# Every third expert row combined in three float32r products, with G built in chunks of 52, 24 and 52 rows

## The chip, the core and the metric

The kernel runs on one core of a Trainium2 chip. The metric is the device time of one launch in microseconds (us). The kernel is one program whose instructions stand in a fixed order on each engine: TensorE (PE in the profile; PEld are its weight loads), VectorE (DVE), ScalarE (ACT), GpSimd (POOL) and SyncE (SP), the last of which issues most DMA transfers. Each engine works through its own list in order and waits on semaphores for the others.

## The reference

Two layers of an encoder work on 512 tokens of width 1024. Each layer has a mixer (attention, a short convolution and a stick-breaking head group) and then a layer of experts; the change lies in the experts. Cut to what matters:

```python
PEER_HEADS, PEER_N_KEYS, PEER_TOPK = 8, 128, 16      # 128 * 128 experts
s1, s2 = scores of two half queries against 128 keys each
top_s, experts = the best 16 of the sums s1 + s2, for each token and head
g = softmax(top_s)
act = gelu(einsum('tkd,td->tk', u_tab[experts], h))   # experts = i1 * 128 + i2
out = einsum('tk,tkd->td', g * act, v_tab[experts])
x   = layer_norm(alpha * x + (1 + gate2) * out)
```

So each token has 8 x 16 = 128 chosen experts out of 16384, each with a row of u and a row of v of 1024 float32 numbers.

## The kernel before

The 512 tokens are four blocks of 128. Two of them (DENSE = 1 and 2, 256 tokens together) compute all 16384 experts, and a table G, which is zero except for a token's chosen experts, keeps those that count. The other two (0 and 3) fetch their chosen rows one by one. Both ways run at the same time, and that stretch is the dense part of a layer.

**The dense blocks** (`dense`, L724 to L885) walk over 128 expert rows; expert row a holds the 128 experts with i1 = a. For each row:

- `load_u` (L801) loads 128 x 1024 numbers of u (512 KB, issued by SyncE), TensorE transposes them in eight pieces into PSUM (L810), ScalarE rounds each half to float32r (`uh`, L812) and VectorE takes the rest (`ul`, L814). A float32r operand holds the leading part of a float32 number.
- `scores` (L819) forms the scores of the row's 128 experts for 256 tokens as a sum over eight pieces of three float32r products each (L824 to L826): high by high, high by low, low by high. ScalarE applies gelu (L828) and VectorE multiplies by G's row (L830); the result is `w` (the tile is named ge).
- `load_v` (L833) loads 512 KB of v.
- `combine` (L839) adds w times v to four PSUM accumulators of 128 x 512 (L842). These four matmuls have float32 operands. A float32 matmul stands in the trace as two records, so a row has eight.

The row loop (L862) emits the transposes of row a + 1, the scores of row a, and the combine of row a - 1, so a combine runs one row behind its scores. The tile v has two buffers: the load of a row's v can start when the combine two rows before is done.

**The table G** is made by `build` (L773). A build covers 8 tokens of one chunk of rows: VectorE makes one-hot tiles of i2 (L781, 1024 elements) and of i1 (L785, 8 x n elements for a chunk of n rows), and multiplies the latter by three parts of g (L790, three times); TensorE joins them in 24 small bf16 matmuls (L797); ScalarE copies the result into G (L799). 256 tokens are 32 builds for a chunk. CUTS sets the chunks: 43, 42 and 43 rows. Two buffers hold G, so a chunk is built while the chunk before it is used: chunk 0's builds stand ahead of row 0; `coming` (L847) spreads chunk 1's 32 builds evenly over rows 0 to 42, and chunk 2's over rows 43 to 84. Rows 85 to 127 have no builds. From chunk 1 on, a build's PSUM tile takes turns with the transposes in two buffers (tag "ut").

**The other blocks** (`experts`, L673) fetch 128 rows at a time with an indirect DMA that GpSimd issues (512 KB a gather, four buffers, L689 and L701). VectorE multiplies and sums each gathered tile of u with h (L691) and adds each gathered tile of v, weighted, to an accumulator (L706).

**What sets the order.** A scheduler orders the instructions of every engine when the program is built. The main loop (L935 to L951) hands it the expert sums in pace with the dense rows: after each row's mark (`held`, the last VectorE instruction of its scores or build) some 2.7 expert sums follow in layer 0 and 2.9 in layer 1, and one after each of chunk 0's builds. On VectorE, expert sums, u's remainders, builds and the gating products thus stand in one list.

Of the kernel before, what the change touches and what calls it, by code (L numbers as in the profile page):

```python
# [11 lines left out]
F32 = mybir.dt.float32  # L12
F32R = mybir.dt.float32r
# [4 lines left out]
OP = mybir.AluOpType  # L18
# [3 lines left out]
P = 128  # L22
D = 1024
# [7 lines left out]
PH, NK, TOPK = 8, 128, 16  # L31
TG = 8
TI = 2
CUTS = (0, 43, 85, 128)
DENSE = (1, 2)
EARLY = (80, 110)
LATE = (50, 0)
# [15 lines left out]
def body(ctx, tc, x, c, positions, ada_w, ada_b, w_in, q_norm_g, kv_norm_g, w_uq, w_ukv, conv_w,  # L53
         w_o, ln1_g, ln1_b, peer_wq, peer_k1, peer_k2, peer_u, peer_v, ln2_g, ln2_b, out):
    nc = tc.nc
# [668 lines left out]
    def dense(y, blocks, res):  # L724
        l = y.l
        st = ExitStack()
        dw = st.enter_context(tc.tile_pool(name=f"dw{l}", bufs=1))
        dps = st.enter_context(tc.tile_pool(name=f"dps{l}", bufs=1, space=PSUM))
        TD = 2 * P
# [36 lines left out]

        NCH = len(CUTS) - 1
        WIDE = max(b - a for a, b in zip(CUTS, CUTS[1:]))
        held = [None]
# [3 lines left out]
        def build(ch, t0):  # L773
            c0, c1 = CUTS[ch], CUTS[ch + 1]
            n = c1 - c0
# [43 lines left out]
        def scores(a, us):  # L819
# [9 lines left out]
            ch = chunk_of[a]  # L829
            held[0] = nc.vector.tensor_tensor(ge, ge, G[ch][:, a - CUTS[ch], :], op=OP.mult)  # L830
            return ge

        def load_v(a):  # L833
# [2 lines left out]
            nc.sync.dma_start(v, v_flat[e0:e0 + NK, :])  # L836
            return v

        def combine(a, w, v):  # L839
            for g in range(2):  # L840
                for i in range(2):
                    nc.tensor.matmul(acc[i][g], lhsT=w[:, i * P:(i + 1) * P], rhs=v[:, g * 512:(g + 1) * 512],  # L842
                                     start=a == 0, stop=a == NK - 1)

        chunk_of = [ch for ch in range(NCH) for _ in range(CUTS[ch], CUTS[ch + 1])]

        def coming(a):  # L847

            ch = chunk_of[a]
            if ch + 1 == NCH:  # L850
                return ch + 1, range(0)
            k, n, m = a - CUTS[ch], CUTS[ch + 1] - CUTS[ch], TD // TG
            return ch + 1, range(k * m // n * TG, (k + 1) * m // n * TG, TG)

        for t0 in range(0, TD, TG):
            build(0, t0)
            yield held[0]
        acc = [[dps.tile([P, 512], F32, name=f"acc{i}{g}", tag=f"acc{2 * i + g}", bufs=1) for g in range(2)]
               for i in range(2)]
        us = load_u(0)  # L860
        w = {}
        for a in range(NK + 1):  # L862
            if a < NK:
                un = load_u(a + 1) if a + 1 < NK else None
                w[a] = scores(a, us)
                us = un
                ch, groups = coming(a)
                for t0 in groups:
                    build(ch, t0)
            if a > 0:  # L870
                combine(a - 1, w.pop(a - 1), load_v(a - 1))
            if a < NK:
                yield held[0]
# [19 lines left out]
    for l in range(L):  # L893
# [40 lines left out]
        res[3] = partial(pick, 3, *h[1:])  # L934
        A.stack.close()  # L935
        dn = dense(y, DENSE, res)
        ex = chain.from_iterable(experts(y, b, *res[b]) for b in range(NB) if b not in DENSE)
        pace(ex, None, EARLY[l])
# [35 lines left out]
```

## Time and profile before

| | us |
|---|---|
| median of three runs | 3543.99 |
| lowest and highest | 3531.81, 3545.16 |
| profiled execution | 3547.72 |
| its span, first to last instruction | 3546.0 |
| TensorE busy in it | 3074.8 |
| VectorE busy in it | 2754.8 |
| ScalarE busy in it | 928.7 |
| GpSimd busy in it | 1456.3 |

Busy is the time in which at least one instruction of the engine ran; on TensorE matmuls overlap, so its pace is better read from the step between the starts of two matmuls. The dense part is the stretch from 671 to 1770 us in layer 0 and from 2421 to 3517 us in layer 1. Its stages below are bounded by the starts of combines: 776.0 is the combine of row 0, 918.7 that of row 16, 1196.6 of row 51, 1389.4 of row 75, and 1770.0 the end of row 127's; in layer 1 row 75's combine stands at 3140.9 and row 127's ends at 3517.2.

### The profile page before, as it was taken

The page shows a single profiled execution, that of the slowest core. Times are in us where ns is not written, and L with a number is a line of the kernel's source. Part 1 is how long each engine was busy: PE and PEld are TensorE (multiplying, and loading weights), DVE is VectorE, ACT ScalarE, POOL GpSimd, SP SyncE. Part 2 cuts the span into 40 slices and gives each one's busy share as a digit, 9 for nine tenths or more (in the row PEclk, how much of TensorE's full clock was granted, in tenths as well). Part 3 has the DMA queues.
Part 4 walks back from the last instruction along what each step waited for, and adds up shares of the span by engine and source line. Part 5 has one row for each costly group of instructions (what it writes and reads, how often), then busy time and mean ns, then how long its engine had stood idle before and what let it go on. Part 6 is the DMA issues. An engine that isn't in the chain of part 4 may idle for free.

```text
span 3546.0 us, 51872 instructions
## 1 busy us (share of the span) xinstructions
PE 3074.8 (87%) x18364; PEld 2019.4 (57%) x18364; DVE 2754.8 (78%) x6213; ACT 928.7 (26%) x1859; POOL 1456.3 (41%) x1347
## 2 busy tenths in 40 slices
PE   7878879659999999999948987785789999999998
PEld 2433434436777777777724444444567767677775
DVE  3667897999777877677675578889998887776777
ACT  2342432222222222222222223312222222222221
POOL 1034563256433434444451144534454444434443
PEclk9989989859999999999969997896799999999998
DMA  8767968558888888899885577794779988889997
GB/s 290 239 206 256 329 227 305 173 192 289 301 325 304 314 308 320 305 343 350 330 296 198 171 273 259 261 325 155 245 275 344 338 309 318 314 323 335 361 352 255
DMA packets 340051, 1011.98 MB, mean 285 GB/s; under 512 B 40504, under 2 KB 53064, under 8 KB 339792
## 3 DMA queue, kind: packets, MB, share of 16 engines
q0 software_dynamic: 147456, 536.94, 42.5%
q1 hardware_dynamic: 192336, 471.73, 38.2%
q8 instruction: 146, 2.39, 0.3%
q14 instruction: 113, 0.93, 0.1%
HBM read 1002.06 MB, written 6.34 MB: 284 GB/s over the span
## 4 chain that ended last, share of the span: by engine, by line
PE 15%; DVE 12%; DMA 10%; issue 9%; POOL 3%; ACT 1%; DVEq 0%; POOLq 0%; ACTq 0%
DMA g<-in_peer_v,eidx 5%; PE acc L842 4%; PE pm L154 3%; DMA g<-in_peer_u,eidx 3%; DVE g L691 2%; DVE acc L706 2%; POOL g L689 2%; PE sp L824 1%; PE sp L825 1%; PE sp L826 1%; DVE tk_ef L661 1%; PE utp L810 1%; POOL g L701 1%; DVE o L790 1%; DVE o L781 1%
## 5 line engine op out<-in xcount | busy, mean ns | idle before, releaser
L701 POOL DMA_INDIRECT g<-in_peer_v,eidx x512 | 613.7, 1199 | 802.2 <-DVE acc L706 486.4
L842 PE MATMUL acc<-v,ge 128*128 128x512 f32 x2048 | 927.1, 595 | 6.8 <-DVE ge L830 6.7
L689 POOL DMA_INDIRECT g<-in_peer_u,eidx x512 | 593.0, 1158 | 755.8 <-DVE g L691 508.5
L706 DVE SCALAR_TENSOR_TENSOR acc<-g,wts,acc 128x1024 f32<-128x1024 f32 x508 | 668.8, 1316 | 143.0 <-DMA g<-in_peer_v,eidx 139.6
L691 DVE SCALAR_TENSOR_TENSOR g<-g,h 128x1024 f32<-128x1024 f32 x512 | 619.7, 1225 | 180.8 <-DMA g<-in_peer_u,eidx 180.2
L824 PE MATMUL sp<-hh,uh 128*128 128x256 f32 x2048 | 613.7, 300 | 1.1 <-ACT ge L828 1.1
L826 PE MATMUL sp<-hh,ul 128*128 128x256 f32 x2048 | 595.0, 291 | 0.0
L825 PE MATMUL sp<-hl,uh 128*128 128x256 f32 x2048 | 584.5, 285 | 0.0
L842 PEld LDWEIGHTS acc<-v,ge 128*128 128x128 f32 x2048 | 370.1, 190 | 372.0 <-issue 364.3
L812 ACT CAST uh<-utp 128x512 fp32r<-128x512 f32 x512 | 303.3, 594 | 911.7 <-PE utp L810 772.6
L814 DVE TENSOR_TENSOR ul<-utp,uh 128x512 fp32r<-128x512 f32 x512 | 346.5, 684 | 106.9 <-ACT uh L812 106.4
L824 PEld LDWEIGHTS sp<-hh,uh 128*128 128x128 f32 x2048 | 392.9, 192 | 6.1 <-issue 4.1
L825 PEld LDWEIGHTS sp<-hl,uh 128*128 128x128 f32 x2048 | 393.1, 192 | 4.6 <-issue 4.5
L826 PEld LDWEIGHTS sp<-hh,ul 128*128 128x128 f32 x2048 | 391.9, 191 | 0.1
L810 PE MATMUL utp<-ident,u 128*128 128x128 f32 x2048 | 304.9, 278 | 57.0 <-DVE ul L814 54.0
L810 PEld LDWEIGHTS utp<-ident,u 128*128 128x128 f32 x2048 | 237.4, 142 | 136.0 <-issue 66.4
L799 ACT COPY G<-pg 128x344 f32<-128x344 f32 (+1 forms) x192 | 146.4, 763 | 561.8 <-PE pg L797 557.9
L797 PE MATMUL pg<-o,o 128*128 128x43 bf16 (+1 forms) x4608 | 182.5, 190 | 97.7 <-DVE o L790 85.4
L797 PEld LDWEIGHTS <-o 128*128 128x128 bf16 x4608 | 162.6, 102 | 179.9 <-issue 84.5
L154 PE MATMUL pm<-wt,hT 128*128 128x512 f32 (+1 forms) x512 | 231.3, 601 | 24.2 <-DMA wt<-in_w_in 13.4
L154 PE MATMUL pm<-wt,h2T 128*128 128x512 f32 x512 | 238.2, 611 | 8.8 <-DMA wt<-in_peer_wq 8.2
L660 POOL TENSOR_TENSOR tk_pick<-tk_hot,tk_ce 128x400 f32<-128x400 bf16 x128 | 125.7, 982 | 153.6 <-DVE tk_hot L658 151.7
(234 smaller groups left out, 3259.9 us busy)
## 6 DMA issues: line engine op xcount, KB each, us to landing
u<-in_peer_u SPq DMA_DIRECT2D x256, 512.0 KB
v<-in_peer_v SPq DMA_DIRECT2D x256, 512.0 KB
wt<-in_peer_wq SPq DMA_DIRECT2D x128, 512.0 KB
adw<-in_ada_w SPq DMA_DIRECT2D x160, 256.0 KB
wt<-in_w_o SPq DMA_DIRECT2D x64, 512.0 KB
wt<-in_w_in SPq DMA_DIRECT2D x48, 512.0 KB
wt<-in_ada_w SPq DMA_DIRECT2D x16, 512.0 KB
g<-in_peer_u,eidx POOLq DMA_INDIRECT x512, 7.0
```

Of the source, the lines that this page charges most:

```text
L154: r = nc.tensor.matmul(pm[:, :n], lhsT=lhsT[:, k0 + k, :], rhs=wt[:, k, :n], start=k0 + k == 0, stop=k0 + k == KT - 1)
L689: nc.gpsimd.indirect_dma_start(out=g, out_offset=None, in_=u_flat, in_offset=bass.IndirectOffsetOnAxis(ap=eidx[:, h, k:k + 1], axis=0))
L691: after(nc.vector.scalar_tensor_tensor(out=g, in0=g, scalar=1.0, in1=h2, op0=OP.mult, op1=OP.mult, accum_out=dots[:, h, k:k + 1]))
L701: nc.gpsimd.indirect_dma_start(out=g, out_offset=None, in_=v_flat, in_offset=bass.IndirectOffsetOnAxis(ap=eidx[:, h, k:k + 1], axis=0))
L706: r = nc.vector.scalar_tensor_tensor(out=acc, in0=g, scalar=wts[:, h, k:k + 1], in1=acc, op0=OP.mult, op1=OP.add)
L797: nc.tensor.matmul(pg[:, tt, 0:n], lhsT=o2[:, tt // TI, :, tt % TI], rhs=o1a[:, tt // TI, p, 0:n, tt % TI], start=tt == 0 and p == 0, stop ...
L810: nc.tensor.transpose(pt[:, j * P:(j + 1) * P], u[:, k * P:(k + 1) * P], ident)
L814: nc.vector.tensor_tensor(ul.rearrange("p j t -> p (j t)"), pt, uh.rearrange("p j t -> p (j t)").bitcast(F32), op=OP.subtract)
L824: nc.tensor.matmul(sp, lhsT=uh[:, j, :], rhs=hh[:, k, :], start=k == 0, stop=False)
L825: nc.tensor.matmul(sp, lhsT=uh[:, j, :], rhs=hl[:, k, :], start=False, stop=False)
L826: nc.tensor.matmul(sp, lhsT=ul[:, j, :], rhs=hh[:, k, :], start=False, stop=k == KT - 1)
L842: nc.tensor.matmul(acc[i][g], lhsT=w[:, i * P:(i + 1) * P], rhs=v[:, g * 512:(g + 1) * 512], start=a == 0, stop=a == NK - 1)
```

## The change

Two things change.

First, CUTS becomes (0, 52, 76, 128): G's chunks are 52, 24 and 52 rows wide. Each still takes 32 builds. Chunk 1's now stand in rows 0 to 51, chunk 2's in rows 52 to 75. A build of a chunk of 52 has 416 elements in its i1 tiles, one of 24 rows 192; before there were 344 or 336.

Second, for rows a with a % 3 == 1 (1, 4, ..., 127: 43 in each layer) `combine` splits w and v into a float32r high part (a copy on ScalarE) and a float32r remainder (a subtraction on VectorE), and replaces each of the four float32 matmuls by three float32r products, high by high, high by low and low by high, as the scores have them. The eight new tiles have one buffer each.

```diff
-CUTS = (0, 43, 85, 128)
+CUTS = (0, 52, 76, 128)
...
+        def split(src, shape, tag):
+            hi = dw.tile(shape, F32R, name="hi", tag=tag, bufs=1)
+            nc.scalar.copy(hi, src)
+            lo = dw.tile(shape, F32R, name="lo", tag=tag + "lo", bufs=1)
+            nc.vector.tensor_tensor(lo, src, hi.bitcast(F32), op=OP.subtract)
+            return hi, lo
+
         def combine(a, w, v):
+            if a % 3 == 1:
+                wh, wl = split(w, [P, TD], "wh")
+                vh, vl = split(v, [P, D], "vh")
+                for g in range(2):
+                    vs = slice(g * 512, (g + 1) * 512)
+                    for i in range(2):
+                        ws = slice(i * P, (i + 1) * P)
+                        nc.tensor.matmul(acc[i][g], lhsT=wh[:, ws], rhs=vh[:, vs], start=False, stop=False)
+                        nc.tensor.matmul(acc[i][g], lhsT=wh[:, ws], rhs=vl[:, vs], start=False, stop=False)
+                        nc.tensor.matmul(acc[i][g], lhsT=wl[:, ws], rhs=vh[:, vs], start=False, stop=a == NK - 1)
+                return
```

The new lines move later ones down: L842 becomes L860, and the new instructions carry L841 (the copies), L843 (the subtractions) and L854 to L856 (the products). The scheduler then orders everything anew.

TensorE, a split row in the second half of layer 0's dense part; acc_6139 to acc_6142 are the four accumulators, u is being transposed at L810. Before:

```order
L826 MATMUL sp<-hh,ul 128x256
L842 MATMUL acc_6139<-v,ge 128x512
L842 MATMUL acc_6141<-v,ge 128x512
L842 MATMUL acc_6140<-v,ge 128x512
L842 MATMUL acc_6142<-v,ge 128x512
L810 MATMUL utp<-ident,u 128x128 x8
```

Now:

```order
L854 MATMUL acc_6139<-hi 128x512
L855 MATMUL acc_6139<-lo,hi 128x512
L856 MATMUL acc_6139<-hi,lo 128x512
L854 MATMUL acc_6141<-hi 128x512
L855 MATMUL acc_6141<-lo,hi 128x512
L856 MATMUL acc_6141<-hi,lo 128x512
L854 MATMUL acc_6140<-hi 128x512
L855 MATMUL acc_6140<-lo,hi 128x512
L856 MATMUL acc_6140<-hi,lo 128x512
L854 MATMUL acc_6142<-hi 128x512
L855 MATMUL acc_6142<-lo,hi 128x512
L856 MATMUL acc_6142<-hi,lo 128x512
```

Four matmuls became twelve between the same neighbours: scores ahead, transposes behind.

VectorE, two rows from the gating product of one (L830) to that of the next but one, around row 58 of layer 0; o with a number are one-hot tiles, 4x86 and 4x104 their four groups of 43 or 52 rows by two tokens. Before:

```order
L830 TENSOR_TENSOR ge<-ge,G 128x256
L781 TENSOR_TENSOR o_11527<-iotab,i2T 128x1024
L785 TENSOR_TENSOR o_11529<-iotab,i1T 128x4x86
L691 SCALAR_TENSOR_TENSOR g,dots<-g,h_10865 128x1024
L790 TENSOR_TENSOR o_11529<-o_11529,gT 128x4x86 x3
L814 TENSOR_TENSOR ul<-utp,uh 128x512 x2
L830 TENSOR_TENSOR ge<-ge,G 128x256
L691 SCALAR_TENSOR_TENSOR g,dots<-g,h_10865 128x1024 x4
L814 TENSOR_TENSOR ul<-utp,uh 128x512
L691 SCALAR_TENSOR_TENSOR g,dots<-g,h_10865 128x1024
L814 TENSOR_TENSOR ul<-utp,uh 128x512
L830 TENSOR_TENSOR ge<-ge,G 128x256
```

Now, the later part of the same stretch:

```order
L781 TENSOR_TENSOR o_11688<-iotab,i2T 128x1024
L785 TENSOR_TENSOR o_11690<-iotab,i1T 128x4x104
L691 SCALAR_TENSOR_TENSOR g,dots<-g,h_10955 128x1024
L843 TENSOR_TENSOR lo<-ge,hi 128x256
L814 TENSOR_TENSOR ul<-utp,uh 128x512
L790 TENSOR_TENSOR o_11690<-o_11690,gT 128x4x104 x3
L814 TENSOR_TENSOR ul<-utp,uh 128x512
L830 TENSOR_TENSOR ge<-ge,G 128x256
L781 TENSOR_TENSOR o_11721<-iotab,i2T 128x1024
L785 TENSOR_TENSOR o_11723<-iotab,i1T 128x4x104
L790 TENSOR_TENSOR o_11723<-o_11723,gT 128x4x104 x3
```

One build in two rows became two whole builds, wider ones, with a split's subtraction among them.

VectorE, one row around row 91 of layer 0, where no builds stand. Before:

```order
L830 TENSOR_TENSOR ge<-ge,G 128x256
L706 SCALAR_TENSOR_TENSOR acc<-g,wts,acc 128x1024 x3
L814 TENSOR_TENSOR ul<-utp,uh 128x512 x2
L830 TENSOR_TENSOR ge<-ge,G 128x256
L706 SCALAR_TENSOR_TENSOR acc<-g,wts,acc 128x1024 x3
```

Now:

```order
L830 TENSOR_TENSOR ge<-ge,G 128x256
L706 SCALAR_TENSOR_TENSOR acc<-g,wts,acc 128x1024
L843 TENSOR_TENSOR lo<-ge,hi 128x256
L706 SCALAR_TENSOR_TENSOR acc<-g,wts,acc 128x1024
L843 TENSOR_TENSOR lo<-v,hi 128x1024
L706 SCALAR_TENSOR_TENSOR acc<-g,wts,acc 128x1024
L814 TENSOR_TENSOR ul<-utp,uh 128x512 x2
L830 TENSOR_TENSOR ge<-ge,G 128x256
```

The two subtractions of a split stand between expert sums, ahead of the remainders of u.

## Rows read from the trace of the kernel before

**Rows 1.** The profile's first line: the span and the number of instructions.

```profile
span 3546.0 us, 51872 instructions
```

**Rows 2.** Combine matmuls (L842) by stage: length, busy us (records) of TensorE.

```profile
918.70:1196.60 277.90, 126.31 (x281) 50.27 (x282) 0.99 0.86 311
1196.60:1389.40 192.80, 87.28 (x192) 34.33 (x193) 1.00 0.87 315
1389.40:1770.00 380.60, 187.63 (x416) 75.15 (x417) 1.00 0.90 332
```

**Rows 3.** Stages: length; busy us; granted clock, DMA share, GB/s.

```profile
core 0: us, PE busy (x) PEld busy (x) DVE busy (x) ACT busy (x) POOL busy (x), PEclk, DMA share, GB/s
671.00:776.00 105.00, 54.10 (x867) 44.70 (x867) 100.63 (x256) 32.13 (x47) 54.17 (x32) 0.60 0.60 193
776.00:918.70 142.70, 128.50 (x904) 93.79 (x905) 130.42 (x285) 34.89 (x63) 77.88 (x64) 0.95 0.83 289
918.70:1196.60 277.90, 270.36 (x2027) 199.59 (x2026) 214.67 (x370) 69.74 (x133) 110.22 (x94) 0.99 0.86 311
1196.60:1389.40 192.80, 187.30 (x1430) 137.96 (x1429) 151.95 (x274) 48.97 (x92) 76.96 (x68) 1.00 0.87 315
1389.40:1770.00 380.60, 375.61 (x2214) 272.57 (x2213) 265.65 (x400) 83.93 (x162) 171.44 (x141) 1.00 0.90 332
3140.90:3517.20 376.30, 373.69 (x2214) 270.86 (x2213) 269.46 (x391) 82.91 (x162) 162.36 (x147) 1.00 0.93 342
```

**Rows 4.** Timeline of TensorE, a row without builds: start, length, engine, line, operation.

```profile
3263.14 3.60 PE L842 MATMUL acc<-v,ge 128*128 128x512 f32 x8
3266.57 1.04 PE L810 MATMUL utp<-ident,u 128*128 128x128 f32 x8
...
3268.05 0.29 PE L826 MATMUL sp<-hh,ul 128*128 128x256 f32 x1
3268.17 0.28 PE L824 MATMUL sp<-hh,uh 128*128 128x256 f32 x1
...
3270.33 1.02 PE L842 MATMUL acc<-v,ge 128*128 128x512 f32 x2
```

**Rows 5.** Timeline of TensorE, the matmuls of one build.

```profile
3012.18 0.78 PE L797 MATMUL pg<-o,o 128*128 128x43 bf16 x24
3012.80 0.64 PE L810 MATMUL utp<-ident,u 128*128 128x128 f32 x4
```

**Rows 6.** Timeline of VectorE while chunk 0 is built.

```profile
743.42 0.67 DVE L781 TENSOR_TENSOR o<-iotab,i2T 128x1024 bf16<-128x1024 bf16 x1
744.02 0.32 DVE L785 TENSOR_TENSOR o<-iotab,i1T 128x344 bf16<-128x344 bf16 x1
744.27 1.27 DVE L706 SCALAR_TENSOR_TENSOR acc<-g,wts,acc 128x1024 f32<-128x1024 f32 x1
745.47 0.82 DVE L790 TENSOR_TENSOR o<-o,gT 128x344 bf16<-128x344 bf16 x3
746.21 0.67 DVE L781 TENSOR_TENSOR o<-iotab,i2T 128x1024 bf16<-128x1024 bf16 x1
```

**Rows 7.** Splits of h by line, 671 to 776 us: busy us, mean ns.

```profile
L741 DVE TENSOR_TENSOR hl<-h2ld,hh 128x1024 fp32r<-128x1024 f32 x2 | 2.4, 1222 | 0.0
L740 ACT CAST hh<-h2ld 128x1024 fp32r<-128x1024 f32 x2 | 2.1, 1045 | 0.8 <-DMA h2ld<-h2scr 0.8
```

**Rows 8.** VectorE by line, 1196.6 to 1389.4 us; last its idle time before, and releaser.

```profile
L706 DVE SCALAR_TENSOR_TENSOR acc<-g,wts,acc 128x1024 f32<-128x1024 f32 x31 | 39.7, 1281 | 15.0 <-DMA g<-in_peer_v,eidx 14.8
L691 DVE SCALAR_TENSOR_TENSOR g<-g,h 128x1024 f32<-128x1024 f32 x32 | 38.5, 1222 | 11.4 <-DMA g<-in_peer_u,eidx 11.4
...
L830 DVE TENSOR_TENSOR ge<-ge,G 128x256 f32<-128x256 f32 x24 | 10.0, 415 | 0.4 <-ACT ge L828 0.3
```

**Rows 9.** DMA, 1389.4 to 1770 us: GB/s in 40 slices; gathers, us to landing.

```profile
GB/s 235 335 365 229 324 306 331 274 218 322 343 373 346 329 361 358 340 326 373 317 371 335 332 369 351 348 341 348 357 325 375 338 332 378 345 324 362 350 275 312
...
g<-in_peer_v,eidx POOLq DMA_INDIRECT x64, 7.0
```

## The prediction

> **What bounds the kernel now.** I read the span [rows 1], then the stages of the dense part with each engine's busy time, then one row of it instruction by instruction on TensorE, then what VectorE runs and waits for. "Row" means expert row, 128 per layer; a stage is counted in rows by its combine matmuls, eight records a row: 281 are 35 rows, 192 are 24, 416 are 52 [rows 2]. The second layer's rows 75–127 are the last line of [rows 3].
>
> The reader should see in [rows 3] that from row 16 on TensorE is busy 270.4 of 277.9 us, 187.3 of 192.8 and 375.6 of 380.6, at a granted clock of 0.99 to 1.00 (the 2.4 GHz level). VectorE has 215 to 266 us of work in the same stretches. So the dense part is TensorE's, except its first stage: while chunk 0 of G is built, VectorE is busy 100.6 of 105.0 us, and TensorE waits at a clock of 0.60. DMA is at 0.86 to 0.93 of its engines.
>
> In a row without builds TensorE has no gap at all [rows 4]: eight combine matmuls from 3263.14 to 3266.57 (3.43 us, 0.429 each), transposes, 24 score matmuls 0.12 apart, the next combine at 3270.33: 7.19 us. A build adds 0.62 us (3012.18 to 3012.80) [rows 5].
>
> VectorE's price is the step from one start to the next, since instructions overlap by some 0.08 us [rows 6]: one-hot of 1024 elements 0.60, of 344 elements 0.25, three products of 344 0.74, one expert sum 1.20. A build of 43 rows so costs 0.60 + 0.25 + 0.74 = 1.59 us.
>
> **Part 1: three products instead of one, 43 rows a layer.** Removed: 8 x 0.429 = 3.43 us of TensorE. Added: 12 float32r matmuls of 512 columns, which no row shows. From above, twice the 256-column step: 0.24. From below: no fixed part can be longer than the shortest matmul step shown, 0.62 / 24 = 0.026 in a build [rows 5], so at least 2 x (0.12 - 0.026) + 0.026 = 0.214. I take the middle, 0.226: 2.71 us, a gain of 0.72 us per split row (0.57 to 0.86), 62 us in the 86 split rows if all of it shows. The Trainium skill ("FP8 and Floating Point Precision", TensorE Precision Notes) says that a true FP32 matmul takes four passes through the array. By that rule a single pass is a quarter of the 0.858 us that the two records of one matmul take, 0.215, and the gain would be 73 us for 62. The trace leans to less, as the 256-column step of 0.12 is more than half of 0.215 [rows 4].
>
> Added on VectorE: two subtractions with both inputs in SBUF. For v the nearest row is the same operation on the same shape, 1.22 us [rows 7], 1.14 as a step; for w the gating product on 256 elements, 0.415 [rows 8], 0.34 as a step: 1.48 us. On ScalarE: 1.05 us [rows 7] and some 0.4; that engine is busy 49 of 193 us [rows 3], so it hides. Loads and their bytes stay.
>
> The new wait: ScalarE's copy of v stands in its queue until v has landed, and VectorE's subtraction behind it; expert sums, and the u splits that TensorE's next scores need, stand behind that. v is asked for when the combine two rows earlier has ended. How long it takes is not shown; a gather of the same 512 KB takes 7.0 us [rows 9]. Copy and subtraction make it 9.2. The combine follows one period and a half later: transposes and scores (3.76), a combine (3.43), transposes and scores again: 10.9 us. So 1.7 us are left, about one late gather.
>
> **Part 2: chunks of 52, 24, 52.** The count of builds stays 32 a chunk. VectorE's slope is (0.60 - 0.25) / 680 = 0.51 ns an element, so the one-hot or product of a 52-row build (416 elements) takes 0.287 and the build 0.60 + 4 x 0.287 = 1.75 us; of a 24-row build (192) 0.172 and 1.29 us. What matters is where they fall: chunk 1's builds, now spread over rows 0 to 51, cost less and are thinner (0.62 a row for 0.74); chunk 2's 32 dear ones all stand in rows 52 to 75 (1.33 a row for 0.76); rows 76 to 127 have none, where before rows 85 to 127 had none.
>
> **The sum, per layer** (layer 0's rows, both layers alike):
> - Chunk 0: 32 x (1.75 - 1.59) = +5 us, on the engine that sets the pace.
> - Rows 0–16: VectorE, busy 130.4 of 142.7, gets 12 x 1.59 - 10 x 1.29 = 6.2 us less of builds and 5 splits, 7.4 us, more. 0 (-4 to +3).
> - Rows 16–51: TensorE 270.4 - 12 x 0.72 - 4.5 x 0.62 = 259; VectorE 214.7 + 12 x 1.48 - (26 x 1.59 - 21.5 x 1.29) = 219. TensorE lies idle 7.5 us now; with splits to wait for I give it 9.5: 268.5, -9 (-13 to +3).
> - Rows 51–75: VectorE 152.0 + (32 x 1.75 - 18.3 x 1.59) + 8 x 1.48 = 190.7; TensorE 187.3 + 13.7 x 0.62 - 8 x 0.72 = 190. Both now equal the old length of 192.8. VectorE's idle time here is 40.9 us, 26.2 of it for gathers [rows 8]. With fewer of its microseconds free between two expert sums, a gather has more work to land behind: in chunk 0's stage, where each sum follows a build, idle is 4.4 of 105 [rows 3]. I keep a quarter of it: 201, +8 (-2 if all goes, +39 if all stays).
> - Rows 75–127: TensorE 375.6 - 7.6 x 0.62 - 17 x 0.72 = 358.7; 3 us for splits that come late make 361.7, -19; in the second layer 373.7 and 376.3 give -16.5. Mean -18 (-22 to -6).
>
> 5 + 0 - 9 + 8 - 18 = -14 a layer, -28 in all. The profiled execution took 3547.7 us (span 3546.0), 3.7 above the median of the runs, 3544.0; I take 28 from the median: 3516 us. So less than half of part 1's 62 us is left, since the builds gather where VectorE can't hide them.
>
> **Rivals.**
> 1. *VectorE takes the lead in rows 52–75, slower.* For it: its work rises from 152 to 191 us there, and an in-order engine that waits for a gather or for v holds up the u splits behind. Against it: in chunk 0's stage it runs nearly without idle time. If all 40.9 us of idle stay: 231.6, +39 for +8, so +17 a layer: +34, 3578 us. It decides once the stage is longer than 215 us.
> 2. *Gathers and loads set the pace outside the builds.* In rows 75–127 DMA already runs at 0.90 and 0.93 of its engines and 332 and 342 GB/s [rows 3]. If faster rows only make gathers later, rows 16–51 give nothing, and rows 75–127 lose their builds (4.7) and idle time (5.0 and 2.6) alone, -9: 5 + 0 + 0 + 8 - 9 = +4 a layer, 3552 us. Against it: pieces of that stretch of 9.5 us reach up to 378 GB/s [rows 9], and VectorE's idle time there is over 100 us a layer.
> 3. *All of part 1 arrives.* Products at 0.214, no new stall: 5 - 3 - 13 - 2 - 24 = -37 a layer, 3470 us. Against it: rows 16–51 already have gaps on TensorE, with VectorE at 77%. The Trainium skill ("SBUF — State Buffer", A bandwidth-pool intuition that's wrong) gives about 358 GB/s between HBM and a core. By that rule the second layer's rows 75–127, at 342 GB/s over 376.3 us, could not go under 359 us, and this rival would end some 7 us later. The trace does not bear it out as a ceiling: pieces of 9.5 us reach 378 [rows 9].
>
> **How the numbers follow.** Forecast 0.53, rival 1 0.17, rival 2 0.20, rival 3 0.10. The forecast's own range is 3490 to 3540. Half a percent (18 us) is what a measurement can tell from no change: faster is below 3526, slower above 3562. Faster takes 0.37 of the forecast, rival 3 and 0.03 of rival 2: 0.50. Same takes 0.16 of the forecast, 0.14 of rival 2 and 0.03 of rival 1: 0.33. Slower 0.17. Range 3470 to 3578, from rival to rival.
>
> **What would show it.** Right: split rows' combine steps of 0.22 to 0.23; rows 76 on at some 6.95 us on average; rows 52–75 at 8.2 to 8.6 us with VectorE above 90% busy; chunk 0's stage 5 us longer. Wrong: split steps at 0.24 or more; TensorE idle ahead of the three products for ScalarE or VectorE, above all where v lands late; rows 76 on still at 7.1 us; the stage of rows 52–75 over 215 us.

## The result and the profile after

The changed kernel took 3496.13 us (median of four runs, 3491.24 to 3500.46); the kernel before, over its four runs, 3544.57 us. The ratio is 0.9875 (95% interval 0.9851 to 0.9899): 48 us less, where 28 were forecast. The profiled execution took 3500.46 us, its span is 3498.7 us, against 3546.0 [rows 1].

The top of the profile after: busy time, share of the span and instructions of each engine.

```profile
span 3498.7 us, 52847 instructions
...
PE 3023.7 (86%) x18708; PEld 2088.1 (60%) x18708; DVE 2871.1 (82%) x6385; ACT 1049.6 (30%) x2031; POOL 1443.6 (41%) x1347
```

TensorE is busy 51 us less and VectorE 116 us more than in the table of before. The time is read by stage again, now bounded by the changed kernel's own combines (781.8, 915.9, 1177.9, 1377.7 and 1737.4 us are the starts of those of rows 0, 16, 51, 75 and 127 in layer 0; layer 1 follows from 2493.5). The columns are those of [rows 3]. The stages of before end in the same place: 1770.0 and 3517.2 are where the combine of row 127 starts, not where it ends, as this row of before shows.

```profile
3517.24 3.67 PE L842 MATMUL acc<-v,ge 128*128 128x512 f32 x8
```

After:

```profile
671.00:781.80 110.80, 59.47 (x871) 48.83 (x871) 109.04 (x271) 37.74 (x51) 54.20 (x32) 0.59 0.61 190
781.80:915.90 134.10, 122.37 (x877) 94.66 (x878) 126.79 (x275) 38.15 (x71) 67.43 (x60) 0.96 0.85 290
915.90:1177.90 262.00, 259.34 (x1978) 205.91 (x1977) 222.00 (x378) 78.57 (x152) 116.15 (x99) 0.99 0.93 339
1177.90:1377.70 199.80, 193.45 (x1774) 154.98 (x1773) 185.22 (x349) 72.02 (x120) 84.64 (x68) 0.99 0.87 302
1377.70:1737.40 359.70, 358.20 (x2114) 279.81 (x2112) 274.86 (x398) 103.86 (x192) 149.80 (x136) 1.00 0.94 344
2493.50:2624.00 130.50, 122.89 (x877) 93.64 (x878) 123.71 (x272) 38.31 (x72) 59.91 (x58) 0.96 0.83 285
2624.00:2885.30 261.30, 259.48 (x1991) 205.65 (x1990) 230.10 (x416) 79.09 (x150) 107.23 (x103) 1.00 0.95 350
2885.30:3091.60 206.30, 195.92 (x1763) 156.74 (x1762) 190.97 (x351) 72.29 (x121) 90.69 (x76) 0.98 0.89 314
3091.60:3451.20 359.60, 358.05 (x2115) 279.88 (x2113) 274.22 (x391) 103.41 (x192) 145.96 (x136) 1.00 0.95 346
3451.20:3498.70 47.50, 11.66 (x42) 5.71 (x42) 39.29 (x47) 2.05 (x4) 19.58 (x18) 0.56 0.53 177
```

Read against [rows 3]: rows 16–51 fell from 277.9 to 262.0 us, and TensorE's gaps there (length less busy) from 7.5 to 2.7. Rows 51–75 grew from 192.8 to 199.8 with VectorE at 185 of them. Rows 75–127 fell from 380.6 and 376.3 to 359.7 and 359.6. The last line is new: from the last combine to the end the changed kernel takes 47.5 us. Before, that stretch was short; it is the last of these lines, which give layer 1 of before from its row 0 on, with rows 75–127 in [rows 3]:

```profile
2524.10:2664.60 140.50, 125.84 (x872) 90.71 (x873) 132.02 (x265) 33.37 (x60) 72.33 (x63) 0.97 0.81 285
2664.60:2946.40 281.80, 272.80 (x2038) 200.79 (x2037) 228.22 (x421) 69.96 (x134) 118.95 (x105) 0.99 0.90 325
2946.40:3140.90 194.50, 187.18 (x1419) 138.38 (x1418) 150.46 (x268) 48.64 (x92) 80.24 (x70) 0.99 0.89 322
...
3517.20:3546.00 28.80, 12.03 (x38) 5.07 (x38) 23.99 (x34) 2.24 (x4) 3.60 (x7) 0.61 0.25 96
```

So the last combine starts 66 us earlier, and the program ends 47 us earlier. What stands in the longer end is read from VectorE's groups by line in it; the first line is of after, the second of before (records, busy us, mean ns, idle time before).

```profile
L706 DVE SCALAR_TENSOR_TENSOR acc<-g,wts,acc 128x1024 f32<-128x1024 f32 x15 | 19.2, 1281 | 1.3 <-DMA g<-in_peer_v,eidx 1.2
```

```profile
L706 DVE SCALAR_TENSOR_TENSOR acc<-g,wts,acc 128x1024 f32<-128x1024 f32 x4 | 5.1, 1280 | 2.2 <-DMA g<-in_peer_v,eidx 2.2
```

Fifteen expert sums instead of four stand behind the dense part: 11 more for 18.7 us more, 1.7 us each. All the runs below with split rows agree: with 8 late sums the end takes 36.2 us, with 10 39.6, with 14 45.6 to 46.7, with 18 53.9 and with 26 or 27 70.0.

A split row in the changed kernel's TensorE timeline, the row that answers to [rows 4]:

```profile
1566.89 3.60 PE L860 MATMUL acc<-v,ge 128*128 128x512 f32 x8
1569.93 0.68 PE L824 MATMUL sp<-hh,uh 128*128 128x256 f32 x1
...
1574.07 1.09 PE L854 MATMUL acc<-hi 128*128 128x512 f32 x4
1575.00 0.39 PE L855 MATMUL acc<-lo,hi 128*128 128x512 f32 x1
1575.23 0.39 PE L856 MATMUL acc<-hi,lo 128*128 128x512 f32 x1
...
1576.59 0.39 PE L856 MATMUL acc<-hi,lo 128*128 128x512 f32 x1
1576.82 0.60 PE L810 MATMUL utp<-ident,u 128*128 128x128 f32 x4
```

Twelve products from 1574.07 to 1576.82 are 2.75 us for 3.43, with no gap ahead of them or between them: 0.68 us gained per split row, some 59 us in 86 if all of it shows. VectorE in rows 51–75 of layer 0, by line, answers to [rows 8]:

```profile
L706 DVE SCALAR_TENSOR_TENSOR acc<-g,wts,acc 128x1024 f32<-128x1024 f32 x32 | 41.0, 1280 | 0.6 <-DMA g<-in_peer_v,eidx 0.5
L691 DVE SCALAR_TENSOR_TENSOR g<-g,h 128x1024 f32<-128x1024 f32 x32 | 38.3, 1222 | 2.0 <-DMA g<-in_peer_u,eidx 2.0
...
L790 DVE TENSOR_TENSOR o<-o,gT 128x416 bf16<-128x416 bf16 x93 | 29.4, 368 | 0.1
...
L843 DVE TENSOR_TENSOR lo<-v,hi 128x1024 fp32r<-128x1024 f32 x8 | 9.8, 1221 | 1.1 <-ACT hi L841 1.0
L843 DVE TENSOR_TENSOR lo<-ge,hi 128x256 fp32r<-128x256 f32 x8 | 3.3, 418 | 0.0
```

The waits for gathers in the last column were 15.0 and 11.4 us and are 0.6 and 2.0: the builds fill the time in which VectorE used to wait for the next gather. Last, what the copy of v and w on ScalarE (L841) waits for and who waits for it, over the whole run (us, times):

```profile
  DMA v<-in_peer_v: 96.8, 53
  DVE ge L830: 81.3, 70
...
  DVE lo L843: 27.9, 31
  PEld acc L854: 2.8, 4
```

The copy stood at the head of ScalarE's list before its v had landed in 53 of 86 split rows. VectorE lies idle for 27.9 us behind the copies of w and v; the waits that the trace puts down to a part of a split on TensorE and its weight loads come to 15 us at most over both layers.

### The profile page after: what moved, and what is told of

Same layout as the page of the kernel before. It is cut to its first block, busy times and chain, and to the rows that moved or that the text cites. A ratio compares the mean times of both kernels' runs of the same rounds, so it can differ in the third digit from the quotient of the medians.

```text
span 3498.7 us, 52847 instructions
## 1 busy us (share of the span) xinstructions
PE 3023.7 (86%) x18708; PEld 2088.1 (60%) x18708; DVE 2871.1 (82%) x6385; ACT 1049.6 (30%) x2031; POOL 1443.6 (41%) x1347
## 4 chain that ended last, share of the span: by engine, by line
PE 49%; DVE 23%; DMA 14%; issue 8%; POOL 3%; ACT 2%; SPq 0%; POOLq 0%; DVEq 0%; ACTq 0%
PE acc L860 12%; PE pm L154 7%; PE sp L826 5%; PE sp L824 5%; PE sp L825 5%; PE utp L810 5%; DMA g<-in_peer_u,eidx 4%; DVE g L691 3%; DMA g<-in_peer_v,eidx 3%; DVE acc L706 3%; DMA adw<-in_ada_w 3%; DVE tk_ef L661 2%; DVE o L790 2%; POOL g L689 2%; PE acc L856 2%
## 5 line engine op out<-in xcount | busy, mean ns | idle before, releaser
L689 POOL DMA_INDIRECT g<-in_peer_u,eidx x512 | 581.2, 1135 | 740.7 <-DVE g L691 510.1
L824 PE MATMUL sp<-hh,uh 128*128 128x256 f32 x2048 | 622.7, 304 | 12.9 <-ACT ge L828 11.5
L860 PE MATMUL acc<-v,ge 128*128 128x512 f32 x1360 | 619.5, 597 | 7.9 <-DVE ge L830 7.9
L860 PEld LDWEIGHTS acc<-v,ge 128*128 128x128 f32 x1360 | 247.4, 191 | 251.5 <-issue 242.5
L810 PE MATMUL utp<-ident,u 128*128 128x128 f32 x2048 | 304.9, 277 | 13.9 <-DVE ul L814 12.5
L797 PE MATMUL pg<-o,o 128*128 128x52 bf16 (+1 forms) x4608 | 189.7, 192 | 102.5 <-DVE o L790 79.3
L799 ACT COPY G<-pg 128x416 f32<-128x416 f32 (+1 forms) x192 | 146.4, 773 | 433.9 <-PE pg L797 395.8
L810 PEld LDWEIGHTS utp<-ident,u 128*128 128x128 f32 x2048 | 239.4, 142 | 61.7 <-issue 33.7
L154 PE MATMUL pm<-wt,hT 128*128 128x512 f32 (+1 forms) x512 | 231.7, 601 | 30.7 <-DMA wt<-in_w_in 18.8
```

The lines of the kernel that those rows point to most:

```text
L154: r = nc.tensor.matmul(pm[:, :n], lhsT=lhsT[:, k0 + k, :], rhs=wt[:, k, :n], start=k0 + k == 0, stop=k0 + k == KT - 1)
L689: nc.gpsimd.indirect_dma_start(out=g, out_offset=None, in_=u_flat, in_offset=bass.IndirectOffsetOnAxis(ap=eidx[:, h, k:k + 1], axis=0))
L797: nc.tensor.matmul(pg[:, tt, 0:n], lhsT=o2[:, tt // TI, :, tt % TI], rhs=o1a[:, tt // TI, p, 0:n, tt % TI], start=tt == 0 and p == 0, stop ...
L810: nc.tensor.transpose(pt[:, j * P:(j + 1) * P], u[:, k * P:(k + 1) * P], ident)
L824: nc.tensor.matmul(sp, lhsT=uh[:, j, :], rhs=hh[:, k, :], start=k == 0, stop=False)
```

## The experiments

Each ratio is to the kernel before in the same session. The kernel before had medians of 3544.57 to 3554.29 us in these sessions, so two experiments are better compared by their ratios than by their medians; a ratio of 0.001 is 3.5 us. The stages of one profiled execution also vary: the way to row 0 of layer 0 with the same builds of 52 rows takes 777.1 to 788.2 us over the runs.

**The chunks alone.** The kernel before with the new chunks, no split rows.

```diff
-CUTS = (0, 43, 85, 128)
+CUTS = (0, 52, 76, 128)
```

> The kernel before with the chunks 52, 24, 52 alone, no split rows. Theory A (the products bring the gain, the chunks cost a little): TensorE has as many builds as before, so only waits change: chunk 0 +5 us a layer, rows 51-75 some +8, rows 75-85 -8 to -10, rows 16-51 -3 to -6; 3540 to 3555 us against 3544, so the split rows alone are worth 45 to 60 us. Rival B (the thinner builds of rows 16-51 bring much of it, since those rows gained 16 and 20 us where 12 splits can explain 8): rows 16-51 shorten by 10 us or more a layer here too, and the whole is 3515 to 3530.

Measured: 3522.35 us, ratio 0.9926 (0.9903 to 0.9948). Its stages in layer 0, then rows 16–51 of layer 1 (columns as in [rows 3]):

```profile
780.50:915.90 135.40, 124.74 (x856) 90.01 (x857) 125.38 (x274) 31.22 (x59) 67.77 (x64) 0.97 0.87 303
915.90:1186.50 270.60, 267.70 (x1930) 197.25 (x1929) 202.30 (x345) 65.90 (x130) 110.08 (x96) 0.99 0.89 323
1186.50:1387.60 201.10, 196.28 (x1742) 147.55 (x1741) 176.58 (x338) 61.66 (x106) 74.98 (x69) 1.00 0.85 300
1387.60:1757.80 370.20, 369.93 (x2047) 267.18 (x2046) 257.40 (x374) 79.19 (x155) 165.03 (x141) 1.00 0.93 341
2648.00:2922.60 274.60, 268.56 (x1942) 196.99 (x1941) 216.34 (x398) 65.55 (x130) 124.25 (x106) 1.00 0.92 335
```

In the total rival B is right: the chunks by themselves gain 26 us by the ratio. Rows 16–51 give less than its 10 us, though, 7.3 and 7.1. Rows 51–75 grow by 8.3 us, and all the other stages of the dense part fall, by 7.2, 7.3 and 10.4. VectorE's waits for gathers in rows 51–75 are 2.3 and 2.7 us here, so the builds by themselves are enough to fill them. With this kernel between the two, each stage's change falls into two parts (us, layer 0 and layer 1; "to row 0" is layer 0's chunk 0 and then the way from layer 0's last combine to layer 1's first, in which layer 1's chunk 0 stands; the parts are of profiled spans, whose sums differ by a few us from what the ratios say):

| stage | forecast per layer | measured | chunks alone | splits on top |
|---|---|---|---|---|
| to row 0 | +5 | +5.7, +2.0 | +4.4, +1.8 | +1.3, +0.2 |
| rows 0–16 | 0 | −8.5, −10.1 | −7.2, −6.2 | −1.3, −3.9 |
| rows 16–51 | −9 | −15.8, −20.5 | −7.3, −7.1 | −8.5, −13.4 |
| rows 51–75 | +8 | +7.0, +11.8 | +8.3, +4.9 | −1.3, +6.9 |
| rows 75–127 | −18 | −20.9, −16.7 | −10.4, −6.8 | −10.5, −9.9 |
| the end | 0 | +18.8 | +1.3 | +17.4 |
| all | −28 | −47 | −24 | −23 |

**No subtractions.** The changed kernel with the high part in place of the remainder.

```diff
-            lo = dw.tile(shape, F32R, name="lo", tag=tag + "lo", bufs=1)
-            nc.vector.tensor_tensor(lo, src, hi.bitcast(F32), op=OP.subtract)
-            return hi, lo
+            return hi, hi
```

> The changed kernel without the two subtractions of a split (the high part stands in for the remainder in the products, so the output lacks the remainders): 43 x 1.48 = 64 us of VectorE less a layer, TensorE's instructions as they are. Theory A (VectorE sets the pace only in rows 51-75 and at the ends): rows 51-75 go from 200 and 206 us to 188 to 194, the other stages by under 3 us; 3465 to 3480 against 3496. Rival B (VectorE's queue delays the splits everywhere): rows 16-51 and 75-127 shorten by 5 us or more each too; under 3460. Rival C (it is hidden): no change, 3490 or more.

Measured: 3473.31 us, ratio 0.9792 (0.9759 to 0.9825). The median is in theory A's range: 118 us less work on VectorE (2753.1 busy for 2871.1) are worth 23 us by the medians, 29 by the ratios. By stage the evidence is thinner, since the profiled execution was the slowest of its runs (3495.2): rows 51–75 shrank in layer 1 alone (190.5 us for 206.3), not in layer 0 (200.0 for 199.8), and the ways to row 0 took 4.8 and 10.7 us more. Fourteen late sums were left and an end of 46.7 us, so VectorE's subtractions are not what makes the sums fall behind.

**Expert sums earlier.** More sums are given to the stretch of layer 1 ahead of its dense part.

```diff
-EARLY = (80, 110)
+EARLY = (80, 122)
```

> The changed kernel with 122 instead of 110 of layer 1's expert sums handed out ahead of the dense part. After the last combine of layer 1 the changed kernel has 15 expert sums left where 4 were left before, and its end takes 47.5 us for 28.8. Theory A (the sums that fell behind cost the end 19 us): with 12 more ahead, the end takes about 30 us and the stretch before the dense part is longer by under 5 us: 3480 to 3486. Rival B (the sums cost the same wherever they stand, or the scheduler lets others fall behind): within 5 us of 3496.

Measured: 3496.51 us, ratio 0.9853 (0.9821 to 0.9885), not to be told from the changed kernel. The end shrank from 47.5 to 39.6 us, with ten late sums for 15, but layer 1's first combine started 12 us later (2505.7 for 2493.5). The cost moved, as rival B has it.

**Every second row split.**

```diff
-            if a % 3 == 1:
+            if a % 2 == 1:
```

> The changed kernel with every second row split (64 rows a layer for 43). Theory A (0.69 us of TensorE per split row where TensorE sets the pace): rows 75-127 go from 360 to about 354 us, rows 16-51 from 262 to 258, rows 51-75 grow by 4 x 1.48 = 6; in all -5 to -10 us, 3486 to 3491. Rival B (the wait for v and VectorE's queue now decide): rows 75-127 don't shorten or grow, 3500 to 3520.

Measured: 3513.07 us, ratio 0.9894 (0.986 to 0.9928). The median is 17 us above that of every third row, but the ratios (0.9894 and 0.9875) are 7 us apart and their intervals overlap: splitting more rows brought nothing, and that it costs something is not shown. From the last combine to the end, and VectorE's sums in it:

```profile
3447.10:3517.10 70.00, 11.36 (x45) 5.78 (x42) 52.31 (x57) 2.05 (x4) 32.59 (x29) 0.54 0.64 207
```

```profile
L706 DVE SCALAR_TENSOR_TENSOR acc<-g,wts,acc 128x1024 f32<-128x1024 f32 x27 | 34.6, 1282 | 10.7 <-DMA g<-in_peer_v,eidx 10.1 <-DVE acc L706 0.2
```

Neither theory holds whole. The dense rows did get shorter, as A says (rows 75–127 353.6 and 353.3 us, rows 85–127 282.8 in both layers for 288.5 and 289.0), but 27 sums and 70 us stand behind them, 22.5 more than in the changed kernel, and the ways to row 0 take 6 and 16 us more. The end was in neither theory.

**Builds of chunk 1 at 52 rows.** The chunks alone, with VectorE's one-hots and products of chunk 1 made 52 rows wide; the added columns are never read.

```diff
-            nc.vector.tensor_tensor(o1a[:, :, 3, 0:n], iotab[:, None, c0:c1].to_broadcast([P, TQ, n, TI]),
+            m = WIDE if ch == 1 else n
+            nc.vector.tensor_tensor(o1a[:, :, 3, 0:m], iotab[:, None, c0:c0 + m].to_broadcast([P, TQ, m, TI]),
...
-                                                   gq.to_broadcast([P, TQ, n, TI]), op=OP.mult)
+                                                   gq.to_broadcast([P, TQ, m, TI]), op=OP.mult)
```

> The chunks 52, 24, 52 without split rows, but VectorE's one-hot and products of chunk 1's builds 52 rows wide as well (columns that nothing reads), so a build of chunk 1 costs VectorE 1.75 us for 1.29 and TensorE the same as with the chunks alone. Chunks alone: 3522 us, ratio 0.9926; TensorE idle in rows 16-51 2.9 and 6.0 us for 7.5 and 9.0 before. Theory A (rows 0-51 gained because VectorE has less to do there): 32 x 0.46 = 15 us of VectorE a layer come back, TensorE's idle time in rows 0-51 rises by 5 to 10 us a layer, ratio 0.995 to 0.999. Rival B (they gained because builds are fewer a row, and each costs TensorE a wait whatever its width): stages as with the chunks alone, ratio 0.991 to 0.994.

Measured: 3537.73 us, ratio 0.9976 (0.9959 to 0.9992), 15 us slower than the chunks alone. Rows 16–51 of both layers, columns as in [rows 3]:

```profile
913.60:1197.90 284.30, 271.57 (x1931) 200.05 (x1930) 211.91 (x346) 65.82 (x130) 112.14 (x96) 0.98 0.86 310
2659.90:2935.80 275.90, 268.64 (x1942) 197.16 (x1941) 224.47 (x396) 65.37 (x129) 124.36 (x105) 1.00 0.92 334
```

Theory A is right: TensorE, which has the same work as with the chunks alone, lies idle 12.7 us in layer 0's stage for 2.9, and over rows 0–51 9.4 us more in layer 0 and 5.9 more in layer 1. Rows 0–51 of both layers took 842.8 us before and 815.0 with the chunks alone; here they take 834.6, so the width of the builds on VectorE gives back 20 of the 28 us. A product of 52 rows takes 369 ns and one of 24 takes 261, so four of them in 32 builds are 14 us of VectorE a layer; 28 us of it in all cost 15 in the median and 20 in the span. In layer 0's stage VectorE was busy only 202 of 271 us, and work added to it still made the stage 13.7 us longer; in layer 1 the same stage grew by 1.3 and rows 0–16 by 5.9. Which waits pass it on is not shown, and layer 1's rows 51–75, whose builds are the same, grew by 6.3 here.

**Sums in pace with the rows.** In VectorE's list a row's gating product does not stand ahead of the sums of the row three before; no wait is added.

```diff
+            if (l, a - 3) in done:
+                tc.add_manual_dep(held[0].ins, done[l, a - 3].ins.name, NOSYNC, reason="expert sums not behind the rows")
```

> The changed kernel, with an order for VectorE's list: a row's gating product may not stand ahead of the expert sums of the row three before (no wait is added, only a place in the list). 9 sums instead of 16 are left behind the last gating product of layer 1. Theory A (the scheduler put the sums too late, and VectorE has room for them in the dense part): the end takes 36 us for 47.5 and the dense part of layer 1 is no longer: 3484 to 3488 against 3496. Rival B (VectorE and its gathers have no room left, so a sum costs about 1.7 us wherever it stands): the dense part grows by what the end gives, 3493 to 3499.

Measured: 3503.37 us, ratio 0.9893 (0.9876 to 0.991), above rival B's range by the median, though the ratio's interval overlaps the changed kernel's. The end fell by 11.3 to 36.2 us with eight late sums, but layer 1's rows 85–127 grew from 289.0 to 296.5 us and its rows 51–75 by 2.3. So what the end gives comes back in the dense part for the most part, as rival B has it, and no time is won.

**A narrower middle chunk,** 57, 14 and 57 rows.

```diff
-CUTS = (0, 52, 76, 128)
+CUTS = (0, 57, 71, 128)
```

> The changed kernel with chunks of 57, 14 and 57 rows: chunk 2's 32 builds all stand in rows 57 to 70. If thin first builds and build-free rows are what gains (theory A): rows 71 to 75 lose their builds as well, rows 57 to 70 take over 10 us each for VectorE's 32 x 1.83 = 59 us of builds in 14 rows; within 10 us of 3496. Rival B (so dense a clump of builds makes VectorE the pace setter for good): 3510 to 3525. It is also the control for three buffers of v.

Measured: 3543.86 us, ratio 1.0008 (0.9991 to 1.0024): all is lost, more than rival B had put. Rows 51–75 took 215.5 and 227.0 us, with 12.5 and 17.6 us of gaps on TensorE.

**The same with three buffers for v** and the tiles that share its tag (three times in the setting up and once in the end as well).

```diff
-            v = dw.tile([P, D], F32, name="v", tag="v", bufs=2)
+            v = dw.tile([P, D], F32, name="v", tag="v", bufs=3)
```

> As the last, chunks of 57, 14 and 57, but v has three buffers for two, so that its load is asked for a row earlier. Theory A (the copy's wait for v, 97 us of ScalarE's idle time in the changed kernel, costs TensorE little: it waited 13 us in all for the parts of w and v): ScalarE's wait for v goes, the time falls by 0 to 8 us against chunks of 57 with two buffers. Rival B (the wait holds up what stands behind it, VectorE's sums and u's remainders, and is why the split rows bring only 22 us of 59): 15 us or more less.

Measured: 3513.75 us, ratio 0.9925 (0.9899 to 0.995), 30 us faster than with two, as rival B has it. ScalarE's wait of the splits for v, with two buffers and then with three (us, times):

```profile
  DMA v<-in_peer_v: 75.5, 48
```

```profile
  DMA v<-in_peer_v: 10.7, 6
```

Rows 51–75 fell to 207.6 and 219.3 us. So with the builds this dense, a third buffer is worth 30 us. Rows 51–75 hold 15.6 of the 36.8 us by which the profiled execution is shorter; 12.0 lie in the ways to row 0, where row 127 of layer 0 is the one split row. Whether the rest comes through the splits or through the plain combines too this run doesn't tell apart. With chunks of 52, 24 and 52 a third buffer wasn't tried: it takes 4 KB more of a partition, and chunks of 57, 14 and 57 have 5 KB less of G.

**No splits in rows 52–75.**

```diff
-            if a % 3 == 1:
+            if a % 3 == 1 and not 52 <= a < 76:
```

> The changed kernel without split rows in rows 52 to 75 (35 splits a layer for 43). There VectorE was busy 185 and 191 of 200 and 206 us. Theory A (the splits bring nothing where builds stand close, since VectorE sets the pace): rows 51-75 don't grow, 8 x 1.48 = 12 us of VectorE a layer leave them; ratio to the changed kernel between 0.995 and 1.001, so 0.983 to 0.9885 against before. Rival B (the products' 0.69 us arrive there too): 16 x 0.69 = 11 us slower, ratio to before 0.990 to 0.992.

Measured: 3487.22 us (3482.94 to 3491.59), ratio 0.9828 (0.9813 to 0.9843): theory A, and a little beyond its range. It beats the changed kernel; the intervals of the two ratios lie apart. Rows 51–75 of both layers:

```profile
1171.60:1373.10 201.50, 196.77 (x1742) 147.77 (x1741) 174.39 (x333) 61.71 (x105) 77.08 (x68) 1.00 0.86 302
2877.60:3078.90 201.30, 196.20 (x1730) 148.08 (x1729) 178.93 (x334) 61.10 (x104) 86.74 (x76) 0.99 0.91 325
```

Without its eight splits TensorE has 8 x 0.68 = 5.4 us more to do there, and the stage is not longer in sum (201.5 and 201.3 for 199.8 and 206.3).

**Splits in pairs two rows apart, then a pause of four.**

```diff
-            if a % 3 == 1:
+            if a % 6 in (1, 3):
```

> The changed kernel with split rows in pairs two apart (a % 6 is 1 or 3), as many as before, 43 a layer. The second of a pair takes the v buffer that the first gave back when it was split, not when its combine ended, so its v is asked for about 7 us earlier. With three buffers of v (chunks of 57, 14 and 57) the time fell by 0.8%. Theory A (that was the wait for v): ScalarE's wait for v falls to about half of 97 us and the ratio to before to 0.982 to 0.986. Rival B (it was the dense clump of builds that made v's wait matter, or two splits close together crowd VectorE): 0.987 or more.

Measured: 3489.62 us, ratio 0.9848 (0.9828 to 0.9868). It is in theory A's range, but its interval overlaps the changed kernel's, and ScalarE's wait for v fell only from 96.8 to 83.4 us. Inconclusive.

**Pairs, and none in rows 48–75.**

```diff
-            if a % 3 == 1:
+            if a % 6 in (1, 3) and not 48 <= a < 76:
```

> Pairs as in the last, and none in rows 48 to 75. Theory A (both help and add up): 0.980 to 0.985 against before, the fastest of the series. Rival B (each is worth nothing by itself, the sums that fall behind set the end): 0.986 to 0.990.

Measured: 3492.71 us, ratio 0.9854 (0.9835 to 0.9873). The two gains do not add up (the ratio lies between what A and B expect), and what the pairs do stays open. Beside the pairs alone (0.9848), leaving the splits out of the middle rows brought nothing here, where it had brought 9 us by the medians, 17 by the ratios, without pairs.

## Why the prediction came right, and where it did not

The direction, and the time to within 20 us (3496 for 3516), came out. That the time came so near is in part luck: rows 0–51 of both layers gained 37 us more than forecast, and the end, which the sum lacks, took 19 of them back. By its own steps:

**The product step** was put at 0.226 us and is 2.75 / 12 = 0.229 in the row shown, 0.23 and 0.22 from one product to the next. The quarter of two records of a float32 matmul, which the Trainium skill's four passes ("FP8 and Floating Point Precision", TensorE Precision Notes) make 0.215, is not reached: 12 products would take 2.57 us, an estimate by that rule. So a split row gains 0.68 us where 0.72 was put.

**VectorE's prices** were right: 1221 and 418 ns for the two subtractions, and one build of chunk 0 in the timeline, which answers to [rows 6], takes 0.60 + 0.29 + 0.86 = 1.75 us without the expert sum in it (1.75 was put):

```profile
738.29 0.70 DVE L781 TENSOR_TENSOR o<-iotab,i2T 128x1024 bf16<-128x1024 bf16 x1
738.89 0.38 DVE L785 TENSOR_TENSOR o<-iotab,i1T 128x416 bf16<-128x416 bf16 x1
739.18 1.29 DVE L706 SCALAR_TENSOR_TENSOR acc<-g,wts,acc 128x1024 f32<-128x1024 f32 x1
740.37 0.95 DVE L790 TENSOR_TENSOR o<-o,gT 128x416 bf16<-128x416 bf16 x3
741.23 0.70 DVE L781 TENSOR_TENSOR o<-iotab,i2T 128x1024 bf16<-128x1024 bf16 x1
```

**The v wait** was priced about right, and a little too dear. From the issue of a split row's v to its first product there are 11.4 us (median of 86 rows; 10.9 was put), and in the 53 rows in which the copy waited it started 6.1 us after the issue (median; 7.0 was put for the landing). That the copy waits is so far no loss, since the first product comes a median of 5.0 us after the copy's start. It reached TensorE for 15 us at most. With chunks of 57, 14 and 57 a third buffer was worth 30 us, but the first-product distance is the same there (11.3 us), so that this margin is the reason is not shown.

**Chunk 0, rows 51–75 and rows 75–127** came near the forecast: +5.7 and +2.0 for +5; +7.0 and +11.8 for +8; −20.9 and −16.7 for −18. One profile doesn't settle a few us of the way to row 0. In rows 75–127 about half of the gain belongs to the chunks, 10.4 and 6.8 us: the sum had 4.7 for the builds, and in layer 0 TensorE's idle time fell from 5.0 to 0.3 as well. Rival 1's point of 215 us was not reached. In rows 51–75 the gather waits shrank, the reason given for keeping a quarter of the idle time.

**Rows 0–16 and 16–51 were mis-sized,** 0 for −8.5 and −10.1, and −9 for −15.8 and −20.5. In rows 16–51 the step "TensorE lies idle 7.5 us now; with splits to wait for I give it 9.5" failed: the gaps fell to 2.7 and 1.8. The thinner builds free VectorE there (the chunks alone, 7 us; the wide builds take most of it back). In rows 0–16 the sum set 7.4 us of splits against 6.2 us of builds on VectorE, but it kept all the expert sums in place. Five of 48 and four of 46 moved on to later rows, some 5 x 1.20 = 6.0 us of VectorE, and the splits cost those rows nothing. The chunks alone, with one sum fewer and one more, gave 7.2 and 6.2 there, as the builds' 6.2 would have it; that the moved sums pay for the splits fits, but no run tests it.

**The end was left out.** The sum took the expert sums as going along with the rows. They fall behind instead: in layer 1 the records of sums in rows 75–127 fell from 147 to 136, and the end has 11 more. That gives back 18.8 us. It comes with the split rows: four sums are late with the chunks alone, 15 with splits on top. But the subtractions on VectorE are not the reason, since 14 are late without them; that shorter rows leave less time for the sums fits the growth from 15 to 27 with every second row split, and is not shown by itself. In the two runs that put sums elsewhere the end shrank by 7.9 and 11.3 us, other stretches grew by about as much, and neither was faster.

**"Less than half of part 1's 62 us is left, since the builds gather where VectorE can't hide them"** is the conclusion that fell. The chunks are no cost but half of the gain, −24 of −47: rows 51–75 hid the builds in what had been waits for gathers, at 5 to 8 us, and all the rows around them became faster, rows 0–51 for the most part because the thinner builds free VectorE, as the wide builds show. The splits' 59 us did shrink, to 23, in another place: some 42 us show in the dense rows, nothing of it net in rows 51–75, and 17 went to the sums at the end.

**Rival 2** had its part: VectorE and the gathers bound the time together with TensorE, though not as it said, in rows 75–127, where the whole gain arrived, but at the end. The Trainium skill's 358 GB/s between HBM and a core ("SBUF — State Buffer", A bandwidth-pool intuition that's wrong) would have kept the second layer's rows 75–127 above 359 us at the old bytes; they took 359.6. No run decides on it: these rows moved 346 GB/s, below that figure, with eleven gathers fewer than before, and with every second row split the same stretch fell to 353.3 us at 343 GB/s. The longest stretch near it is 350 GB/s over 261 us.

**Open:** how much the late v costs at chunks of 52, 24 and 52; what pairs of splits do; what puts the sums behind; and the split rows with the old chunks, which weren't tried, so that "on top" is measured in one order only. The two parts of the change are tied by memory: a row of G takes 1 KB of a partition (256 tokens of 4 bytes), so two buffers of 52 and 24 rows take 9 KB less than 43 and 42, and a split's four tiles take 10 KB.

## What to carry to other kernels

Price a change that moves work by stage, and put the moved work where an engine already waits for something else: 32 builds put into 24 rows cost those rows 5 to 8 us a layer, and the chunks alone still gained 24. Where two engines and the DMA bound a stretch together, follow the work that has no fixed place (here the expert sums) to the end of the program, since what a faster stretch leaves undone is paid there, at 1.7 us a sum here. Spend a second engine's time only in stages where it buys something: leaving the splits out of rows 52–75 made the kernel faster by 9 us by the medians and 17 by the ratios, though with splits in pairs the same omission brought nothing.

## What the runs showed of the hardware

A float32r matmul of 512 columns steps at 0.22 to 0.23 us, a little under two of 256 columns (0.12), and three of them beat the two records of one float32 matmul (0.858) by 20%. While both transfers and matmuls ran densely, DMA moved 350 GB/s over 261 us at 0.95 of its engines' time, where before no stage was above 342.
